# Probabilities turned, attention and spatial gating moved to joint places between the gate blocks of a macaron decoder layer

## The chip, the cores and the metric

The kernel runs on one core of a Trainium2 chip. The metric is the device time of one execution in microseconds (us); of several executions the median is given. A profile is one execution with the hardware profiler on; its span runs from the first to the last instruction.

## What is computed

A layer of a decoder on 256 tokens of 1024 features, in float32: a SwiGLU feed-forward, a token mixer with two branches, a second feed-forward and a last norm. Only the mixer matters here:

```python
n = rmsnorm(h, mix_norm[l])
z = n @ w_in[l]                                  # q, k, v, and the two halves of the gating
attn = moba_attention(q, k, v)                   # 8 heads of 64, causal softmax over 256 keys
gm = chunked_spatial_gating(zg[..., :512], zg[..., 512:], ln_g, ln_b, w_s, b_s)
y_attn = attn @ w_branch_attn[l]
y_gmlp = gm @ w_branch_gmlp[l]
gates = jax.nn.sigmoid(n @ w_gate[l] + b_gate[l])
merged = gates[..., :D] * y_attn + gates[..., D:] * y_gmlp
h = h + merged @ w_out[l]
```

## The kernel before, in words

**Products.** Every float32 weight is split into a high and a low part of 12 significant bits (`split`: a cast on ACT, L176, and a subtraction on DVE, L177), and so are the activations; a product is high x high, high x low and low x high. `by_weights` makes one block of 128 features for all 256 tokens: eight steps over the 1024 input features, each of two matmuls in `mm_side`, one of 512 columns (L159, both activation parts side by side) and one of 256 (L155). Its result is one PSUM bank with two sides. `collect` adds the sides: ACT copies one side to a small buffer `lo` (L172, two such buffers), and DVE adds the other to it (L173). Only then is the bank free.

**Banks.** All results in PSUM come from one pool, `psum`, of eight banks with one tag: `bank(name)` hands them out in turn, so each tile waits until the tile eight before it has been read.

**Weights** come in units of 1 MB, each loaded in two halves by SP into a ring of three raw buffers, split, and kept in a ring of five split units; `unit(i)` asks for loads up to three units ahead.

**Order.** The order on PE and on SP is the order of the program's text, written by hand. On DVE, ACT and POOL a scheduler sets the order; each engine then works strictly in that order.

**The stage around the change.** The scores of both token tiles (six banks `sc`, L468) come first. DVE adds the causal mask (L475) and finds the maxima (L478), ACT takes the exponentials (L483, 8 for tile 0 and 8 for tile 1), and DVE scales them by the reciprocal sums (L486, L488) in place: the probabilities. Meanwhile PE begins the sixteen gate blocks, f = 0 to 15: `gate_block(f)` is one `by_weights` (tile `pgate`), a `collect` into `gz`, a scaling (L495) and a sigmoid (L496). Between the gate blocks the loop puts smaller work on PE:

- `spatial(gp)`, gp 0 to 3: four small float32 matmuls into one bank `mix` (L532), then on DVE the bias (L535) and the product with u (L538) and a `split` into `gmT`.
- `turn(hp)`, hp 0 to 3 (two heads each): six transposes of probabilities into two banks `pk` (L505 to L507), which ACT (L509) and DVE (L511) copy to two tiles `pT`.
- `attend(hp)`: eight products of `pT` with the values into one bank `po` (L520, L522), then a `split` into `aoT`.

Before, `spatial` stood behind gates 1, 3, 5 and 7, `turn(0)` ahead of gate 7, and `attend(hp)` with `turn(hp + 1)` behind gates 8, 10 and 12; `attend(3)` stood between gates 14 and 15. The branches (L553 on) follow gate 15: for each of eight blocks one bank `pb`, its left half from `aoT` (twelve matmuls), its right half from `gmT` (twelve), then the two products with the gates, their sum and a `split`.

Of the kernel before, what the change touches and what calls it, by code (L numbers as in the profile page):

```python
# [18 lines left out]
P = 128  # L19
# [22 lines left out]
def block_kernel(ctx, tc, t, out):  # L42
# [12 lines left out]

    # The residual stream, tokens on partitions.
    h = act.tile([P, NT, D], F32, tag="h", name="h")
# [5 lines left out]

    # Until it comes, the first block of the transposed input, behind the first norm's gains.
    x0 = h[:, 0, :KB + S]
# [5 lines left out]
    eps = consts.tile([P, 1], F32, name="eps")  # L71
    nc.vector.memset(eps, EPS)
    # The activation table and the tensor engine's clock come up while the first loads run.
    warm = small.tile([P, 1], F32, tag="warm", name="warm", bufs=1)
# [6 lines left out]

    # ---- weights: loaded once, in the order in which they are used, and split
    # exactly into two float32r parts of 12 significant bits each.
    units = []
# [27 lines left out]

    # The first units wait for their split where the first hidden layer will be.
    staging = [act.tile([P, FB, S], F32, tag=f"aT{p}", name=f"stage{p}") for p in "hl"]
# [9 lines left out]
    def load_rows(i, k, end):  # L124
        """Rows k..end of a unit, loaded and split."""
        name, u = units[i]
        raw = (stage(i, k, end - k) if i < STAGED else
               rawp.tile([P, end - k, t[name].shape[-1]], F32, tag="raw", name=f"raw{i}_{k}"))
        nc.sync.dma_start(raw, t[name][u][:, k:end, :])
        w = parts[i]  # L130
        split(w[:, k:end, 0, :], w[:, k:end, 1, :], raw)
# [12 lines left out]

    # ---- float32 products of parts: high x high, high x low and low x high.
    def mm_side(ps, st, both, first, last):
        """ps[:, :n] takes high x high, ps[:, n:] the two mixed products.

        both: the moving operand's parts side by side."""
        sh, sl = st  # L150
        n = both.shape[-1]
        m = both.rearrange("p two n -> p (two n)")

        def low():
            nc.tensor.matmul(ps[:, n:], sl, both[:, 0, :], start=False, stop=False)  # L155

        if last:
            low()
        nc.tensor.matmul(ps, sh, m, start=first, stop=last)  # L159
        if not last:  # L160
            low()
# [7 lines left out]
    def collect(to, ps):  # L169
        """The sum of the sides of mm_side's bank."""  # L170
        lo = tmp.tile([P, S], F32, tag="lo", name="lo")
        nc.scalar.copy(lo, ps[:, S:])  # L172
        nc.vector.tensor_add(to, ps[:, :S], lo)  # L173
# [5 lines left out]
    def alloc_T(name, tags):  # L179
        """Feature-major activations of 1024 features: two tiles of four blocks, each in parts."""  # L180
        return [act.tile([P, 4, 2, S], F32R, tag=tag, name=f"{name}{c}") for c, tag in enumerate(tags)]
# [7 lines left out]
    def put_T(nT, src, j, half):  # L189
        """Features 4*half.. of one token tile's [P, 512] src into nT."""  # L190
        ps = bank(f"tr{j}{half}")
        for b in range(4):
            nc.tensor.transpose(ps[:, b * P:(b + 1) * P], src[:, b * P:(b + 1) * P], ident)
        tk = slice(j * P, (j + 1) * P)
        split(nT[half][:, :, 0, tk], nT[half][:, :, 1, tk], ps.rearrange("p (b t) -> p b t", b=4))
# [9 lines left out]
    def square_sum(hh, j, hf, name):  # L205
        """The sum of squares of half of each token's features."""
        if hf == 0:
            sums[name, j] = small.tile([P, 2], F32, tag="ss", name=f"ss{name}{j}")
        sq = tmp.tile([P, 512], BF16, tag="sq", name=f"sq{name}{j}{hf}", bufs=1)
        nc.scalar.activation(sq, hh[:, j, hf * 512:(hf + 1) * 512], AF.Square,  # L210
                             accum_out=sums[name, j][:, hf:hf + 1])

    def rstd_of(j, name):
        """1 / sqrt(mean(x^2) + eps) of each token of a tile."""
        ss = sums.pop((name, j))
        ms = small.tile([P, 1], F32, tag="ms", name=f"ms{name}{j}")
        nc.vector.tensor_add(ms, ss[:, 0:1], ss[:, 1:2])
        nc.vector.tensor_scalar(ms, ms, 1.0 / D, EPS, op0=ALU.mult, op1=ALU.add)
        r = small.tile([P, 1], F32, tag="rstd", name=f"rstd{name}{j}")
        nc.gpsimd.tensor_tensor(r, ms, nhalf, op=ALU.pow)  # L220
        return r

    def rows_of(rs, name):
        """The tokens' factors along the free axis, on every partition."""
        ps = bank(f"rows{name}")
# [6 lines left out]
    def by_weights(name, i, nT, blk):  # L232
        """A bank's two sides of [feature, token], 128 columns of unit i."""
        ps, w = bank(name), unit(i)
        c = slice(blk * P, (blk + 1) * P)
        for k in range(KB):
            mm_side(ps, (w[:, k, 0, c], w[:, k, 1, c]), both_of(nT, k), k == 0, k == KB - 1)
        return ps

    def by_tokens(name, i, nT, j):  # L240
        """A bank's two sides of [token, column], unit i for token tile j."""
        ps, w = bank(name), unit(i)
# [7 lines left out]
    def down(i0, n_units, part_of, scale, hh, name, done, put=None, following=(), cuts=(HALVES, HALVES)):  # L250
        """hh + scale * (a @ w), one token tile after the other at the end.

        done(new, j, cut) follows each cut of a token tile's features, put(j, cut) turns
        it over for the next product, whose first matmuls are in following."""
        acc = {(j, c0): bank(f"acc{name}{j}{c0}") for j in range(NT) for c0, n in cuts[j]}
# [38 lines left out]
    def gate_up(aT, gu, rows, name, f):  # L294
        """aT block f of silu(g) * u; g and u lie side by side in gu, to be scaled by rows."""
        nc.vector.tensor_mul(gu, gu, rows[:, None, :].to_broadcast([P, 2, S]))  # L296
# [12 lines left out]

    # ---- first feed-forward  # L310
    nT = alloc_T("n1", ("nA", "nB"))
# [15 lines left out]

    # The first units come block after block with the input.
    for i in range(2):
# [31 lines left out]

    # Constants of the mixing layer.
    bgate = consts.tile([P, 2 * KB], F32, name="bgate")
# [17 lines left out]
    def to_norm(nT, gain, rs, name):  # L381
        """What follows the parts of the residual stream on their way into the next norm."""
        hg = {}
# [18 lines left out]

    # ---- mixing
    mix_a = act.tile([P, FB, S], F32, tag="aTh", name="mix_a")
# [50 lines left out]

    # Scores of each token tile against the keys up to its own, and their softmax.
    for j in range(NT):
# [4 lines left out]
        for a0 in range(0, HEADS // 2, per):  # L462
            # Heads of different rows of the array write different banks.
            pair = [bank(f"sc{j}{a0}{two}") for two in range(2)]
# [24 lines left out]

    # Gates: sigmoid(n @ w_gate + b), features on partitions.  # L490

# [8 lines left out]
    def turn(hp):  # L500
        """The probabilities of heads 2*hp and 2*hp+1, keys on partitions."""
        pk0, pk1 = bank(f"pk0{hp}"), bank(f"pk1{hp}")
# [11 lines left out]
    def attend(hp, t0, t1):  # L514
        """The heads' probabilities times their values."""
        po = bank(f"po{hp}")
# [9 lines left out]
    def spatial(gp):  # L526
        """Groups 2*gp and 2*gp+1 of the gating, both chunks."""
        ps = bank(f"mix{gp}")
# [10 lines left out]
        split(gmT[:, gp, 0, :], gmT[:, gp, 1, :], m2)  # L539

    for f in range(2 * KB):
        if f >= 7 and f % 2 == 1 and f < 15:
            turned = turn((f - 7) // 2)
        gate_block(f)
        if f >= 8 and f % 2 == 0:
            attend(f // 2 - 4, *turned)
        if f % 2 == 1 and f < 8:
            spatial(f // 2)

    # Branches, merged by the gates.  # L550
    mT = alloc_T("mg", ("nA", "nB"))
    for f in range(KB):
        i = mb + 2 * (f // 4)  # L553
        ps = bank(f"pb{f}")
        c = slice(f % 4 * P, (f % 4 + 1) * P)
        for q, bT in enumerate((aoT, gmT)):
            w = unit(i + q)
# [23 lines left out]

    # ---- second feed-forward and the last norm
    aT, aT_block = ffn_alloc("f2")
# [21 lines left out]
    def done3(new, j, i):  # L605
        c0, n = last_cuts[j][i]
        sl = slice(c0, c0 + n)
        if i == 0:
            o[j] = act.tile([P, 2 * D], F32, tag=f"n{'CD'[j]}", name=f"o{j}")
        # Squares of x / 32: their sum is the mean over the 1024 features.  # L610
        ss = small.tile([P, 1], F32, tag="ss", name=f"ss4{j}{i}")
# [24 lines left out]
def _packed(inputs):  # L636
    """The inputs, each weight laid out unit after unit as the kernel loads it."""
    def cols(w, k, c):
# [47 lines left out]
```

## Time and profile before

| what | before |
|---|---|
| time, median of 3 runs | 556.17 us (551.77 to 558.6) |
| span of the profiled execution | 553.5 us |
| PE busy in it | 539.8 us (98%) |
| DVE busy | 394.1 us (71%) |
| ACT busy | 308.4 us (56%) |
| DMA, mean | 186 GB/s |

The profile gives the profiled execution's span alone, 553.5 us, with no time of its own around it; it lies within the runs shown. Each engine has its own queue and works it in order; a wait of PE is shown behind its row as `[idle before <-releaser]`. Matmuls overlap: the time that one adds is the distance between the starts of two rows, not the length of one.

### The profile page before, as it was taken

What the parts mean: (1) busy time and instruction counts of PE and PEld (TensorE: products, weight loads), DVE (VectorE), ACT (ScalarE), POOL (GpSimd) and SP (SyncE); (2) the same over time, 40 slices, a digit from 0 to 9 for tenths busy, and PEclk for the clock granted to TensorE, in tenths of its full rate; (3) what the DMA queues carried; (4) which work ended last, traced back from release to release, by engine and by line L of the source; (5) the groups of instructions that cost most, each with busy time, mean ns of one, the idle gap of its engine ahead of it and who ended that gap; (6) DMA issues with size and microseconds to landing.
All of it is one profiled execution on the core that took longest, in us unless ns stands there. A gap on an engine that the chain in (4) does not pass through costs nothing.

```text
span 553.5 us, 8102 instructions
## 1 busy us (share of the span) xinstructions
PE 539.8 (98%) x3042; PEld 464.2 (84%) x3042; DVE 394.1 (71%) x623; ACT 308.4 (56%) x541; POOL 10.8 (2%) x25
## 2 busy tenths in 40 slices
PE   7999999999999899999999999999999999999995
PEld 5888888888888788888878898888888888888884
DVE  5688888767745674887888777778787787866304
ACT  6666666555544454645977634575555655554203
POOL 0000000000000010000000000000000000000002
PEclk9999999999999999999999999999999999999999
DMA  8756675656767636556146545555655456556302
GB/s 254 316 174 213 210 236 178 194 181 212 252 225 235 221 125 225 188 188 206 60 142 209 183 142 196 197 190 185 200 189 187 153 178 204 195 188 229 111 0 77
DMA packets 30150, 103.03 MB, mean 186 GB/s; under 512 B 3488, under 2 KB 4256, under 8 KB 30112
## 3 DMA queue, kind: packets, MB, share of 16 engines
q1 hardware_dynamic: 30112, 102.52, 56.1%
q8 instruction: 24, 0.39, 0.3%
q14 instruction: 14, 0.11, 0.1%
HBM read 101.46 MB, written 1.05 MB: 185 GB/s over the span
## 4 chain that ended last, share of the span: by engine, by line
PE 49%; DMA 23%; DVE 15%; ACT 8%; issue 3%; SPq 1%; POOL 0%; POOLq 0%; DVEq 0%; ACTq 0%
DVE w L177 8%; PE f2u L159 7%; PE f2g L159 7%; DMA raw<-in_f1g 6%; ACT w L176 6%; DMA raw<-in_f1d 6%; PE acch L165 5%; PE acch L166 5%; PE acch L167 5%; DMA raw<-in_gate 4%; PE f2u L155 4%; PE f2g L155 4%; DMA raw<-in_qk 3%; PE pgate L159 2%; PE f L159 2%
## 5 line engine op out<-in xcount | busy, mean ns | idle before, releaser
L177 DVE TENSOR_TENSOR w<-raw,w 128x1024 fp32r<-128x1024 f32 x176 | 212.9, 1222 | 87.1 <-ACT w L176 86.5
L176 ACT CAST w<-raw 128x1024 fp32r<-128x1024 f32 x176 | 182.2, 1051 | 108.5 <-DMA raw<-in_f1d 17.6
L159 PE MATMUL f2g<-n,w 128*128 128x512 f32 x160 | 58.4, 399 | 0.0
L159 PE MATMUL f2u<-n,w 128*128 128x512 f32 x160 | 58.1, 397 | 0.0
L159 PE MATMUL f1g<-n,w 128*128 128x512 f32 x144 | 52.5, 399 | 0.0
L159 PE MATMUL f1u<-n,w 128*128 128x512 f32 x144 | 52.4, 397 | 0.0
L159 PE MATMUL pgate<-n,w 128*128 128x512 f32 x128 | 46.5, 405 | 0.7 <-DVE uz L173 0.7
L298 ACT ACTIVATE sgf<-guf 128x256 f32<-128x256 f32 x38 | 15.9, 417 | 48.3 <-DVE guf L296 48.3
L155 PE MATMUL f2u<-n,w 128*128 128x256 f32 x160 | 41.7, 281 | 0.0
L155 PE MATMUL f2g<-n,w 128*128 128x256 f32 x160 | 41.6, 281 | 0.0
L166 PE MATMUL acch<-w,f2h 128*128 128x512 f32 (+1 forms) x110 | 38.3, 349 | 0.0
L165 PE MATMUL acch<-w,f2h 128*128 128x512 f32 (+1 forms) x110 | 38.3, 348 | 0.0
L167 PE MATMUL acch<-w,f2l 128*128 128x512 f32 (+1 forms) x110 | 38.1, 347 | 0.0
L155 PE MATMUL f1u<-n,w 128*128 128x256 f32 x144 | 37.6, 281 | 0.0
L155 PE MATMUL f1g<-n,w 128*128 128x256 f32 x144 | 37.5, 281 | 0.0
L159 PEld LDWEIGHTS f2u<-n,w 128*128 128x128 f32 x160 | 30.2, 189 | 5.4
L159 PEld LDWEIGHTS f2g<-n,w 128*128 128x128 f32 x160 | 30.1, 188 | 5.5
L165 PE MATMUL acch<-w,f1h 128*128 128x512 f32 x88 | 34.3, 390 | 0.0
L167 PE MATMUL acch<-w,f1l 128*128 128x512 f32 x88 | 34.2, 389 | 0.0
L166 PE MATMUL acch<-w,f1h 128*128 128x512 f32 x88 | 34.2, 389 | 0.0
L155 PE MATMUL pgate<-n,w 128*128 128x256 f32 x128 | 33.3, 281 | 0.0
L155 PEld LDWEIGHTS f2u<-n,w 128*128 128x128 f32 x160 | 30.2, 189 | 1.9
(191 smaller groups left out, 1101.8 us busy)
## 6 DMA issues: line engine op xcount, KB each, us to landing
raw<-in_f1d SPq DMA_DIRECT2D x22, 512.0 KB, 4.6
raw<-in_f2g SPq DMA_DIRECT2D x22, 512.0 KB, 3.8
raw<-in_f2u SPq DMA_DIRECT2D x22, 512.0 KB, 4.9
raw<-in_f2d SPq DMA_DIRECT2D x22, 512.0 KB, 4.1
raw<-in_f1g SPq DMA_DIRECT2D x18, 512.0 KB, 4.6
raw<-in_f1u SPq DMA_DIRECT2D x18, 512.0 KB, 4.8
raw<-in_gate SPq DMA_DIRECT2D x16, 512.0 KB, 4.8
raw<-in_qk SPq DMA_DIRECT2D x8, 512.0 KB, 5.7
```

Of the source, the lines that this page charges most:

```text
L155: nc.tensor.matmul(ps[:, n:], sl, both[:, 0, :], start=False, stop=False)
L159: nc.tensor.matmul(ps, sh, m, start=first, stop=last)
L165: nc.tensor.matmul(ps, sh, mh, start=first, stop=False)
L166: nc.tensor.matmul(ps, sh, ml, start=False, stop=False)
L167: nc.tensor.matmul(ps, sl, mh, start=False, stop=last)
L176: nc.scalar.copy(hi, src)
L177: nc.vector.tensor_sub(lo, src, hi.bitcast(F32))
L298: nc.scalar.activation(sg, gu[:, 0, :], AF.Silu)
```

## The change

The four `spatial` calls go to two places: 0 and 1 ahead of gate 2, 2 and 3 ahead of gate 4. `turn(0)` goes from ahead of gate 7 to ahead of gate 8, and the pairs `attend(hp)`, `turn(hp + 1)` from behind gates 8, 10, 12 to ahead of gates 10, 12, 14, one block later each; `attend(3)` stays between gates 14 and 15. In the branches the `gmT` half is multiplied first. Nothing is added to or taken from the computation. (The diff also drops comments and docstrings, which shifts line numbers behind L540 by 8.)

```diff
+    turned = {}
+
+    def turn_next(hp):
+        turned[hp] = turn(hp)
+
+    def attend_next(hp):
+        attend(hp, *turned.pop(hp))
+
+    between = {2: [(spatial, 0), (spatial, 1)], 4: [(spatial, 2), (spatial, 3)], 8: [(turn_next, 0)],
+               10: [(attend_next, 0), (turn_next, 1)], 12: [(attend_next, 1), (turn_next, 2)],
+               14: [(attend_next, 2), (turn_next, 3)], 15: [(attend_next, 3)]}
     for f in range(2 * KB):
-        if f >= 7 and f % 2 == 1 and f < 15:
-            turned = turn((f - 7) // 2)
+        for step, i in between.get(f, ()):
+            step(i)
         gate_block(f)
-        if f >= 8 and f % 2 == 0:
-            attend(f // 2 - 4, *turned)
-        if f % 2 == 1 and f < 8:
-            spatial(f // 2)
...
-        for q, bT in enumerate((aoT, gmT)):
+        for q, bT in ((1, gmT), (0, aoT)):
             w = unit(i + q)
```

On PE, gates 1 to 5 before (the first row of a block stands for its sixteen matmuls; `x4` is the four matmuls of one `spatial`; the number behind a name only keeps tiles apart):

```order
L159 MATMUL pgate1_2553<-n21_1466,w43_2258 128x512
L532 MATMUL mix0_2575<-wsT_1457,mix_a_1948 64x128 x4
L159 MATMUL pgate2_2587<-n20_1465,w44_2332 128x512
...
L159 MATMUL pgate3_2619<-n20_1465,w44_2332 128x512
...
L532 MATMUL mix1_2641<-wsT_1457,mix_a_1948 64x128 x4
L159 MATMUL pgate4_2653<-n20_1465,w45_2387 128x512
...
L159 MATMUL pgate5_2685<-n20_1465,w45_2387 128x512
...
L532 MATMUL mix2_2707<-wsT_1457,mix_a_1948 64x128 x4
```

and after:

```order
L159 MATMUL pgate1_2553<-n21_1466,w43_2258 128x512
L532 MATMUL mix0_2575<-wsT_1457,mix_a_1948 64x128 x4
L532 MATMUL mix1_2586<-wsT_1457,mix_a_1948 64x128 x4
L159 MATMUL pgate2_2598<-n20_1465,w44_2332 128x512
...
L159 MATMUL pgate3_2630<-n20_1465,w44_2332 128x512
...
L532 MATMUL mix2_2652<-wsT_1457,mix_a_1948 64x128 x4
L532 MATMUL mix3_2663<-wsT_1457,mix_a_1948 64x128 x4
L159 MATMUL pgate4_2675<-n20_1465,w45_2387 128x512
```

Counted from gate 0, the ninth bank asked for was that of `mix2`, behind gate 5; now it is that of gate 4.

On DVE, ahead of and at the copy of turned probabilities that `attend(0)` needs (`pT10`), before:

```order
L173 TENSOR_TENSOR gz4_2652<-pgate4_2653,lo_2679 128x256
L173 TENSOR_TENSOR gz5_2684<-pgate5_2685,lo_2702 128x256
L495 TENSOR_TENSOR gz4_2652<-gz4_2652,rowsb2_2099 128x256
L177 TENSOR_TENSOR ag1_2519<-gm1_2648,ag1_2519 128x256
L495 TENSOR_TENSOR gz5_2684<-gz5_2684,rowsb2_2099 128x256
L535 TENSOR_TENSOR mixb2_2712<-mix2_2707,bs_1454 128x256
L177 TENSOR_TENSOR w49_2720<-raw49_4_2725,w49_2720 128x4x256
L538 TENSOR_TENSOR gm2_2714<-mixb2_2712,mix_b_1949 128x256
L173 TENSOR_TENSOR gz6_2718<-pgate6_2719,lo_2745 128x256
L511 COPY pT10_2760<-pk10_2751 128x256
```

and after:

```order
L538 TENSOR_TENSOR gm3_2670<-mixb3_2668,mix_b_1949 128x256
L495 TENSOR_TENSOR gz4_2674<-gz4_2674,rowsb2_2099 128x256
L173 TENSOR_TENSOR gz5_2706<-pgate5_2707,lo_2724 128x256
L177 TENSOR_TENSOR w50_2798<-raw50_0_2799,w50_2798 128x4x256
L177 TENSOR_TENSOR ag1_2519<-gm3_2670,ag1_2519 128x256
L495 TENSOR_TENSOR gz5_2706<-gz5_2706,rowsb2_2099 128x256
L173 TENSOR_TENSOR gz6_2729<-pgate6_2730,lo_2756 128x256
L511 COPY pT10_2794<-pk10_2785 128x256
```

The copy still stands right behind the collect of gate 6 (`gz6`), but all four `spatial` results and one more half unit of weights (`w50`) are now ahead of it. From the collect of gate 0 (`gz0`) to this copy DVE had four weight splits and 21 smaller instructions; it now has five and 25. Ahead of `gz0` DVE and ACT have the same instructions in the same order as before.

## Rows read from the trace of the kernel before

**Rows 1.** The page: span, and engines by busy time, share and instructions.
```profile
span 553.5 us, 8102 instructions
PE 539.8 (98%) x3042; PEld 464.2 (84%) x3042; DVE 394.1 (71%) x623; ACT 308.4 (56%) x541; POOL 10.8 (2%) x25
```

**Rows 2.** Who PE waited for, two of seven: us in total, times, longest.
```profile
PE tr L193 <- DVE hg L200: 1.6, 2, 0.9
...
PE pgate L159 <- DVE uz L173: 0.7, 1, 0.7
```

**Rows 3.** Timeline of PE, gates 0 to 4: start, length, instruction.
```profile
260.26 0.63 PE L159 MATMUL pgate<-n,w 128*128 128x512 f32 x2
...
263.08 0.39 PE L159 MATMUL pgate<-n,w 128*128 128x512 f32 x1
263.40 0.66 PE L532 MATMUL mix<-wsT,mix_a 128*64 128x128 f32 x8
263.99 0.50 PE L159 MATMUL pgate<-n,w 128*128 128x512 f32 x1
...
269.82 0.66 PE L532 MATMUL mix<-wsT,mix_a 128*64 128x128 f32 x8
270.41 0.50 PE L159 MATMUL pgate<-n,w 128*128 128x512 f32 x1
```

**Rows 4.** Timeline of PE around `attend(0)`, `attend(1)` and `attend(3)`.
```profile
286.96 0.40 PE L159 MATMUL pgate<-n,w 128*128 128x512 f32 x1
287.65 0.65 PE L520 MATMUL po<-pT,mix_b 128*64 128x256 f32 x2 [0.29 <-ACT pT L509]
289.11 0.32 PE L522 MATMUL po<-pT,mix_b 128*64 128x128 f32 x1 [0.81 <-DVE pT L511]
...
290.54 0.47 PE L159 MATMUL pgate<-n,w 128*128 128x512 f32 x1
...
296.02 0.39 PE L159 MATMUL pgate<-n,w 128*128 128x512 f32 x1
...
297.78 0.47 PE L159 MATMUL pgate<-n,w 128*128 128x512 f32 x1
...
310.91 0.66 PE L520 MATMUL po<-pT,mix_b 128*64 128x256 f32 x4
```

**Rows 5.** Timeline of DVE: collects of gates 0 and 1, splits, copies, a branch.
```profile
275.24 0.75 DVE L173 TENSOR_TENSOR gz<-pgate,lo 128x256 f32<-128x256 f32 x2
...
276.57 2.36 DVE L177 TENSOR_TENSOR w<-raw,w 128x1024 fp32r<-128x1024 f32 x2
...
288.63 0.42 DVE L511 COPY pT<-pk 128x256 f32<-128x256 f32 x1
...
307.77 0.42 DVE L511 COPY pT<-pk 128x256 f32<-128x256 f32 x1
...
323.49 0.42 DVE L561 TENSOR_TENSOR m<-pb,mix_a 128x256 f32<-128x256 f32 x1 [0.77 <-PE pb L167]
```

**Rows 6.** Windows: busy PE, PEld, DVE, ACT, POOL; granted PE clock; DMA share, GB/s.
```profile
12.00:16.00 4.00, 4.00 (x17) 3.44 (x16) 3.69 (x8) 3.04 (x7) 0.00 (x0) 0.57 1.04 412
...
192.00:196.00 4.00, 3.30 (x18) 2.71 (x19) 3.71 (x8) 2.86 (x7) 0.55 (x1) 1.00 0.36 122
...
548.00:552.00 4.00, 0.00 (x0) 0.00 (x0) 0.90 (x3) 0.80 (x3) 0.74 (x2) 0.92 0.34 131
```

**Rows 7.** Timeline of PE in the first feed-forward's first blocks (`f`).
```profile
10.34 0.50 PE L159 MATMUL f<-n,w 128*128 128x512 f32 x1 [2.56 <-ACT w L176]
...
13.02 0.41 PE L155 MATMUL f<-n,w 128*128 128x256 f32 x1
...
13.66 0.41 PE L155 MATMUL f<-n,w 128*128 128x256 f32 x1
...
15.87 0.28 PE L155 MATMUL f<-n,w 128*128 128x256 f32 x1
...
16.21 0.28 PE L155 MATMUL f<-n,w 128*128 128x256 f32 x1
```

## The prediction

> **What bounds the kernel now.** I read the page first: PE is busy 98% of the 553.5 us span, DVE 71%, ACT 56% [rows 1]. So PE sets the time, and what matters is only how long PE stands still or works more slowly. Second I read the list of what PE waited for. It has seven rows. Two name weights, and both lie in the first blocks of the first feed-forward; from there on PE never waits for a weight. The two waits at the turns into a new norm, 1.6 us together [rows 2], follow from PE's own work and move with it. So whatever PE gains or loses among the gates reaches the end of the kernel in full. Third I read PE's timeline through the gates. The places where the loop leaves the gate blocks show as steps in the starts, and two waits stand at `attend(0)` [rows 4]. Fourth I read DVE over the same stretch, for the time at which it frees PE's banks [rows 5], and last the granted clock in windows, since a longer wait of PE can lower it [rows 6, 7].
>
> **The joint places.** The unbroken step from the last matmul of one gate to the next is 0.23 us: the pair of rows at 260.26 is 0.63 long where one alone is 0.40 [rows 3]. From the last matmul of gate 1 (263.08) to the first of gate 2 (263.99) it is 0.91, so a `spatial` with its two changes of work costs 0.68. Its eight matmuls take 0.66 in all, 0.27 of it the last one's length (the row's 0.66 against steps of about 0.056), so the second `spatial` in a place adds 8 x 0.056 = 0.45, not 0.68. Two places are saved: 2 x 0.23 = **-0.46 us**. `turn` and `attend` stand in as many places as before (five), so they give nothing here.
>
> **The bank of gate 4.** The pool has eight banks in turn. That a tile really waits for the eighth before it shows at gate 0, which waited 0.7 us for DVE to collect a `pu` block [rows 2]: two `pu`, six `sc`, gate 0. Counted from gate 0, the ninth tile was `mix2`; PE came to it only after gate 5, when the collect of gate 0 was over. Now the first eight are gates 0 to 3 and all four `mix`, and the ninth is gate 4. PE gets there early. Gate 2 starts 0.45 later than at 263.99, at 264.44; gates 2 and 3 take the 5.83 us from 263.99 to 269.82 [rows 3], so `mix2` starts at 270.27; 0.59 (269.82 to 270.41) and 0.45 more, and gate 4 is due at 271.31. The collect of gate 0 starts at 275.24 and takes 0.42 [rows 5]. It stands behind the softmax, and nothing ahead of it on DVE or ACT has moved, nor waits for PE: the bank is free at 275.66. A wait of PE ends about 0.06 later (the copy from 288.63 to 289.05 released the row at 289.11 [rows 4, 5]). PE waits from 271.31 to 275.72: **+4.41 us**. Behind gate 4 stands everything on PE. Gates 5, 6 and 7 need the banks of gate 1 and of the first two `mix`, which DVE reads within some 4 us of 275.24, ahead of PE.
>
> Here a rule speaks the other way. Perfetto Trace Analysis in the Trainium skill, section Optimizing Tensor Performance, Matmuls, says that independent groups should rotate through different banks, so that the evacuation of one overlaps the next group's matmuls. The kernel still rotates; by the rule alone the 4.41 would be nothing and the sum -2.28. The rows show that rotation hides an evacuation only as long as the ring holds a free bank, and here it comes round 4.4 us too soon.
>
> **The wait at `attend(0)`.** From the last matmul of gate 8 (286.96, plus the step of 0.23) to the first of gate 9 (290.54) `attend(0)` and `turn(1)` took 3.35 us; the same pair after gate 10, without a wait, took 297.78 - 296.25 = 1.53 [rows 4]. So the wait, for copies that came at 288.63 on DVE, cost 1.82. After the change DVE has five weight splits (1.14 apart: two in 2.36, of which the last is 1.22) and 25 small ones (0.33 apart) from `gz0` to that copy, 13.95 us, which is 289.2 without a wait. Before, four and 21 made 11.5, and the copy came 1.9 later than that [rows 5]; with the same delay it now starts at 291.1. PE comes to `attend(0)` after six gates (2.92 each, from the 5.83) and one turn from 275.72: not before 293.2. So the copy is in time: **-1.82 us**. If DVE falls behind by 2 us more, this is lost, up to 1.82.
>
> **`attend(3)`** now follows its `turn` by one gate instead of two. Before, it started at 310.91 without a wait, so its turn ended at about 310.91 - 5.83 = 305.1; the copy ended at 308.19 [rows 4, 5], 3.1 after it. One gate covers 2.92. I take **0**; the bounds are 0 and the 1.82 of `attend(0)`.
>
> **The clock.** The trace shows one wait of PE like the new one: 2.56 us before 10.34 [rows 7]. From about 12 on the granted clock is at its lower level: the window 12 to 16 has a mean of 0.57, which is (1 - 0.57) / 0.5 x 4 = 3.4 us at 1.2 instead of 2.4 GHz [rows 6]. In it a pair of matmuls took 0.64 (13.02 to 13.66), afterwards 0.34 (15.87 to 16.21) [rows 7]. 3.4 / 0.64 = 5.3 pairs, 0.30 each: 1.6 us. The 1.6 us of waits at the turn into the second norm did not lower it (1.00 from 192 to 196), and after PE's end it fell at about 551.4, over 3.4 us into the idle time [rows 6]. A wait of 4.41 is far longer than the one that sufficed, so I expect a fall near its end or shortly after: **+1.6 us**. Bounds: 0 if it doesn't fall; 1.1 if the fall comes 3.4 us into the wait, so that 1.0 of the low stretch is waited away; 3.2 if it stays low for two stretches.
>
> **The branches.** `gmT` first: the matmuls are the same, in another order; PE did not wait for `aoT` before, and DVE began with a `pb` block only after both halves (the wait of 0.77 before 323.49 [rows 5]). A unit of the attention branch is now given back twelve matmuls later, which delays the split of an output weight by 1.4 us, with units split well ahead of use. **0**; what hides it is that lead, and if that were gone the cost would be up to 1.4 for each of two units.
>
> **Sum:** -0.46 + 4.41 - 1.82 + 0 + 1.6 + 0 = **+3.7 us**. Against the profiled execution's own span, 553.5, this is 557.2. The median of the runs is 556.17, 2.7 above that span; single runs go from 551.77 to 558.6. On the median the forecast is **559.9 us**, 0.7% slower.
>
> **The rivals.**
> 1. *The stall without the clock's fall*: +2.1, 558.3. For it: clock 1.00 through every other wait after 16 us. Against it: 2.56 us sufficed once. Chance 0.17.
> 2. *Stall, clock, and late copies*: `attend(0)` still waits its 1.82, or `attend(3)` waits as long: +5.5, 561.7. For it: DVE's extra split and the short way to `attend(3)`. Against it: PE comes later, DVE works on while PE waits. Chance 0.13.
> 3. *Faster: no stall at gate 4.* If the collect of gate 0 were done when PE arrives, -0.46 - 1.82 = -2.3 remains: 553.9. The point that decides is a wait at gate 4 of under 2.28 us, so a collect over by 273.5 instead of 275.66 (and a wait so short may leave the clock alone). For it: the softmax chain ahead of the collect varies with the landing of a weight half. Against it: nothing of the change is ahead of it. Chance 0.08.
> 4. *Nothing happens*, as the stall replaces what `attend(0)` lost or is made up later: 556.2. Against it: 4.41 against 2.28, and no later wait of PE that a delay could shorten. Chance 0.04.
>
> The forecast itself has 0.58. About 2% (11 us) is what a measurement of this kernel can tell from no change. No case reaches that: the worst, 4.41 - 0.46 + 3.2 + 1.82 + 1.4, is +10.4. So same 0.96, slower 0.03, faster 0.01. For the range I take rivals 1 and 2 at its inner side, with about 3 us for the scatter that the runs before show about their median: 555.5 to 563.5. Rival 3 lies below it.
>
> **What the profile after would show.** A wait of PE ahead of gate 4 of about 4.4 us, released by DVE's collect of `gz` (L173); a `spatial` place with sixteen matmuls in about 1.1 us; no wait at `attend(0)`; a window of 3 to 4 us with the clock near 0.5 beginning near 275 to 279; the branches at the same 2.9 us a block; gate 0 to the first branch matmul 3.7 us longer than before. The prediction is wrong if gate 4 starts near 271.3 on the old scale, if the clock stays at 1.00, or if PE waits at `attend(3)`.

## The result, and the profile after

The changed kernel takes 558.2 us (median of 20 runs, 555.35 to 560.99); the kernel before took 555.29 in the same rounds. The ratio is 1.0059, with a 95% interval of 1.004 to 1.0078. Run twice more the same code gave 1.0052 and 1.0039 (below). So the change costs 0.4 to 0.6%, some 2 to 3 us: well under 2%, but clearly above nothing. The forecast was 559.9 us, 3.7 above before; rival 1, the stall without the clock's fall, stood at 558.3, so the time alone does not part the two. (Ratios are of undisturbed runs alone, so a median below stands a little off its ratio here and there.)

| what | before | after |
|---|---|---|
| median of 20 runs each | 555.29 us | 558.2 us |
| span of the profiled execution | 553.5 us | 553.3 us |
| wait of PE ahead of gate 4, in it | none | 1.29 us |
| gate 0 to the first branch matmul, in it | 57.1 us | 55.5 us |
| matmuls of `spatial` in one place, first start to last end | eight, 0.66 us | sixteen, 1.09 us |

The page of the profiled execution after, span and engines, answers to [rows 1]:

```profile
span 553.3 us, 8106 instructions
PE 538.5 (97%) x3042; PEld 463.8 (84%) x3042; DVE 394.2 (71%) x623; ACT 308.6 (56%) x541; POOL 10.6 (2%) x25
```

That span is not longer than before's. It belongs to the fastest of the 20 runs (555.35 us; a run's time is its span and 2.0 to 2.1 us in each of them), so this one trace cannot show the typical loss. Its list of what PE waited for (us in total, times, longest) has a row that before lacked, the third of these:

```profile
PE tr L193 <- DVE hg L200: 3.6, 2, 2.9
PE f L159 <- DVE n L325: 2.2, 1, 2.2
PE pgate L159 <- DVE gz L173: 1.3, 1, 1.3
```

The timeline of PE through gates 0 to 4 after (start, length, instruction) answers to [rows 3], and around `attend(0)` to [rows 4]:

```profile
258.78 0.50 PE L159 MATMUL pgate<-n,w 128*128 128x512 f32 x1
...
264.60 1.09 PE L532 MATMUL mix<-wsT,mix_a 128*64 128x128 f32 x16
265.62 0.50 PE L159 MATMUL pgate<-n,w 128*128 128x512 f32 x1
...
271.45 1.09 PE L532 MATMUL mix<-wsT,mix_a 128*64 128x128 f32 x16
273.83 0.50 PE L159 MATMUL pgate<-n,w 128*128 128x512 f32 x1 [1.29 <-DVE gz L173]
...
291.61 0.66 PE L520 MATMUL po<-pT,mix_b 128*64 128x256 f32 x4
```

The joint places stand there as sixteen matmuls in 1.09 us. Gate 4 waits for the collect of gate 0's bank, as the prediction said, but for 1.29 us and not 4.41. `attend(0)` begins without a wait; its four matmuls come in one piece. The collect on DVE and the granted clock in that stretch (windows: PE busy, clock, DMA share, GB/s) answer to [rows 5] and [rows 6]:

```profile
273.36 0.75 DVE L173 TENSOR_TENSOR gz<-pgate,lo 128x256 f32<-128x256 f32 x2
```

```profile
258.00:274.00 16.00, 14.71 (x105) 1.00 0.28 92
274.00:278.00 4.00, 4.00 (x23) 1.00 0.24 70
```

The collect starts 14.58 us behind gate 0 (258.78 to 273.36). In before's trace it started 17.67 behind it. And the clock stayed at its upper level after this wait.

The third run of the same code was profiled in an execution of about the median time. There PE's timeline, DVE's, and the windows read:

```profile
256.88 0.50 PE L159 MATMUL pgate<-n,w 128*128 128x512 f32 x1
...
269.55 1.09 PE L532 MATMUL mix<-wsT,mix_a 128*64 128x128 f32 x16
274.14 0.50 PE L159 MATMUL pgate<-n,w 128*128 128x512 f32 x1 [3.49 <-DVE gz L173]
...
275.04 0.41 PE L155 MATMUL pgate<-n,w 128*128 128x256 f32 x1
...
275.68 0.41 PE L155 MATMUL pgate<-n,w 128*128 128x256 f32 x1
...
279.17 0.28 PE L155 MATMUL pgate<-n,w 128*128 128x256 f32 x1
...
279.52 0.28 PE L155 MATMUL pgate<-n,w 128*128 128x256 f32 x1
```

```profile
273.66 0.75 DVE L173 TENSOR_TENSOR gz<-pgate,lo 128x256 f32<-128x256 f32 x2
```

```profile
274.00:278.00 4.00, 3.86 (x13) 0.57 0.15 42
278.00:282.00 4.00, 4.00 (x25) 1.00 0.67 223
```

This is the picture of the prediction: a wait of 3.49 us for the collect of gate 0, not quite the 4.41, and soon after gate 4 begins the clock falls to 1.2 GHz. A pair of matmuls takes 0.64 (275.04 to 275.68) instead of 0.35 (279.17 to 279.52). (1 - 0.57) / 0.5 x 4 is 3.4 us at the lower level. From gate 0 to the first branch matmul this execution needs 59.2 us.

### The profile page after: what moved, and what is told of

It reads as the page before. It is cut to its first block, busy times and chain, and to the rows that moved or that the text cites. A ratio compares the mean times of both kernels' runs of the same rounds, so it can differ in the third digit from the quotient of the medians.

```text
span 553.3 us, 8106 instructions
## 1 busy us (share of the span) xinstructions
PE 538.5 (97%) x3042; PEld 463.8 (84%) x3042; DVE 394.2 (71%) x623; ACT 308.6 (56%) x541; POOL 10.6 (2%) x25
## 3 DMA queue, kind: packets, MB, share of 16 engines
q1 hardware_dynamic: 30112, 102.52, 55.5%
## 4 chain that ended last, share of the span: by engine, by line
PE 81%; DMA 7%; DVE 6%; ACT 3%; issue 1%; SPq 0%; POOL 0%; POOLq 0%; DVEq 0%; ACTq 0%
PE acch L165 8%; PE acch L166 8%; PE acch L167 8%; PE f2g L159 7%; PE f2u L159 7%; PE f1g L159 6%; PE f1u L159 6%; PE pgate L159 4%; PE f2g L155 4%; PE f2u L155 4%; DMA raw<-in_qk 3%; PE f1u L155 3%; PE f1g L155 3%; DVE w L177 3%; DMA raw<-in_gate 2%; PE f L159 2%
```

## The experiments

Three theories were put against each other. By the *ring theory*, that of the prediction, the loss is the wait of gate 4 for gate 0's bank and the clock that falls in it. By the *late-turns theory* it is `turn` and `attend` standing a block later. By the *chance theory* the clock falls at places that have nothing to do with the gates. "Low-clock time" is worked out from each run's span and mean granted clock c as 2 (1 - c) x span: the time at 1.2 GHz when the rest is at 2.4. It is given over the runs that the ratio counts. A run's mean clock does not say where in the kernel the clock fell; that only a trace shows.

| kernel | median us | runs | ratio to before, 95% | low-clock us, mean |
|---|---|---|---|---|
| changed, first | 558.20 | 20 | 1.0059 [1.004, 1.0078] | 10.6 |
| changed, again | 557.95 | 12 | 1.0052 [1.0018, 1.0087] | 10.3 |
| changed, third | 557.06 | 12 | 1.0039 [1.0017, 1.006] | 9.7 |
| gatings joined alone | 556.16 | 12 | 1.0024 [0.9988, 1.006] | 9.0 |
| turns late alone | 555.73 | 12 | 1.0047 [1.0006, 1.0089] | 7.0 |
| changed, gatings at gates 6 and 7 | 555.38 | 12 | 0.9997 [0.9962, 1.0032] | 5.2 |
| changed, paired halves of a bank | 553.67 | 12 | 0.9993 [0.9964, 1.0023] | 6.2 |
| the same again | 555.62 | 12 | 0.9979 [0.9943, 1.0015] | 6.3 |
| paired halves, turns as before | 554.54 | 12 | 0.9973 [0.994, 1.0006] | 7.0 |
| changed, the wait filled | 556.05 | 12 | 1.0022 [0.9991, 1.0053] | 5.2 |
| before, ring shortened by two | 559.24 | 12 | 1.0044 [1.0005, 1.0082] | 7.9 |
| changed, ring shortened by three | 562.27 | 6 | 1.0112 [1.0071, 1.0154] | 14.6 |
| before, against itself | 554.19 | 12 | 1.0018 [0.999, 1.0047] | 5.3 |

The kernel before has a mean of 6.7 us of low-clock time over 108 runs, those of the last row among them. The last row says how far a ratio can be from 1 by chance here: differences of 0.002 are not to be read. Low-clock time scatters too: before has 6.8 to 7.0 in three sets of runs and 5.3 in the fourth. Behind the first row there are three sets of runs of before. Beside the first stood the changed kernel again, the two halves and the late gatings; beside the second the changed kernel's third run, the first of the paired halves, the filled wait and before itself; beside the third the two shortened rings, the paired halves again and those with the turns as before.

**The changed kernel again, and its two halves.**

> The changed kernel once more, for a second trace of it and the granted clock of every run. Ring theory (mine): gate 4 is the ninth bank of the ring and waits for the collect of gate 0; the first trace of the changed kernel, its fastest execution, showed 1.3 us of that wait at clock 1.00, so slower executions must show a longer one (up to 4.4 us) and, where it is long, a stretch of 3.4 us at the lower clock behind it: ratio to before 1.006, mean clock of the slow runs 0.003 below that of the fast ones for each such stretch. Rival (late-turns theory: the delay comes from turn and attend standing a block later and from attend(3) only one gate behind its turn): waits at po, none over 1.5 us at gate 4, ratio 1.006. Rival (chance theory: the clock falls elsewhere, at the turn into the second norm, as in that first trace): before has as many runs at a lowered clock as this.

> Only the four spatial calls stand in their two joint places; turn, attend and the order of the branch halves are those of before. Ring theory: the ninth bank is that of gate 4 as in the change, so the wait at gate 4 and the fall of the clock stay; attend(0) keeps its 1.8 us at most: ratio 1.006 to 1.010 (+3.5 to +5.5 us). Late-turns theory: nothing of the delay is here: ratio 0.999 (-0.5 us). Chance theory: ratio 0.999 to 1.001.

```diff
-    between = {2: [(spatial, 0), (spatial, 1)], 4: [(spatial, 2), (spatial, 3)], 8: [(turn_next, 0)],
-               10: [(attend_next, 0), (turn_next, 1)], 12: [(attend_next, 1), (turn_next, 2)],
-               14: [(attend_next, 2), (turn_next, 3)], 15: [(attend_next, 3)]}
+    between = {2: [(spatial, 0), (spatial, 1)], 4: [(spatial, 2), (spatial, 3)], 7: [(turn_next, 0)],
+               9: [(attend_next, 0), (turn_next, 1)], 11: [(attend_next, 1), (turn_next, 2)],
+               13: [(attend_next, 2), (turn_next, 3)], 15: [(attend_next, 3)]}
...
-        for q, bT in ((1, gmT), (0, aoT)):
+        for q, bT in enumerate((aoT, gmT)):
```

> Only turn and attend stand a block later, as in the change; spatial 0 to 2 stand as before, spatial 3 ahead of gate 8 beside turn(0); the branch halves in the order of before. Ring theory: mix2 behind gate 5 is the ninth bank as before, no wait at gate 4; the 1.8 us at attend(0) go: ratio 0.9965 (-2.0 us). Late-turns theory: the whole delay is here: ratio 1.006. Chance theory: 0.9965 to 1.

```diff
-    between = {2: [(spatial, 0), (spatial, 1)], 4: [(spatial, 2), (spatial, 3)], 8: [(turn_next, 0)],
+    between = {2: [(spatial, 0)], 4: [(spatial, 1)], 6: [(spatial, 2)], 8: [(spatial, 3), (turn_next, 0)],
...
-        for q, bT in ((1, gmT), (0, aoT)):
+        for q, bT in enumerate((aoT, gmT)):
```

The changed kernel repeated its ratio here, and once more in its third run (expected below). Its trace had a wait of 0.86 us ahead of gate 4 and no fall of the clock. The halves went against the ring theory: 1.0024 with the gatings alone, where it had 1.006 to 1.010, and 1.0047 with the turns alone, where it had 0.9965, below the whole interval. Both intervals hold what the late-turns theory expected (0.999 and 1.006). They are wide and overlap, and with the turns alone the medians differ by 0.6 us only (555.73 against 555.10), so the ratios of the halves settle nothing. But their traces differ. With the gatings alone PE's timeline and the windows show the wait and the fall once more:

```profile
268.22 1.09 PE L532 MATMUL mix<-wsT,mix_a 128*64 128x128 f32 x16
271.79 0.50 PE L159 MATMUL pgate<-n,w 128*128 128x512 f32 x1 [2.47 <-DVE gz L173]
```

```profile
271.00:273.00 2.00, 1.22 (x7) 1.00 0.00 0
273.00:277.00 4.00, 4.00 (x16) 0.57 0.44 135
```

With the turns alone there is no wait at the gates, and from gate 0 to the first branch matmul it takes 55.7 us, against 58.1 with the gatings alone. Its low-clock time is that of before (7.0), while the gatings alone have 9.0.

**The gatings late.** The changed kernel with the joint places ahead of gates 6 and 7, so that the ninth bank comes later.

> The changed kernel with its two joint places of spatial moved back: 0 and 1 ahead of gate 6, 2 and 3 ahead of gate 7. Ring theory: the first eight banks are those of gates 0 to 5 and two mix, the ninth is that of gate 6, which PE reaches at about 276, when the collect of gate 0 is over: no wait there, clock 1.00, and the joint places and attend(0) keep their gain: ratio 0.996 (-2.3 us). Late-turns theory: the delay stays: ratio 1.006. Chance theory: 0.996 to 1.

```diff
-    between = {2: [(spatial, 0), (spatial, 1)], 4: [(spatial, 2), (spatial, 3)], 8: [(turn_next, 0)],
+    between = {6: [(spatial, 0), (spatial, 1)], 7: [(spatial, 2), (spatial, 3)], 8: [(turn_next, 0)],
```

The loss is gone from the ratio (0.9997) with the turns left late, and the low-clock time is back, though the 0.996 that the ring theory had did not come. Its trace shows no wait at gates 6 and 7, but one behind them, for a bank of a gating:

```profile
284.28 0.50 PE L159 MATMUL pgate<-n,w 128*128 128x512 f32 x1 [0.84 <-DVE mixb L535]
```

With this and late copies at `attend(0)`, `attend(2)` and `attend(3)` that execution takes 57.8 us from gate 0 to the first branch matmul, so the one trace is not free of loss. The run speaks for the ring, but it moves the gatings too; the next one moves nothing on PE.

**Paired halves.** TensorE's order is that of the changed kernel, matmul for matmul; two gatings share a bank.

> The changed kernel, except that the two spatial gatings of a joint place write the two halves of one bank instead of a bank each. TensorE's order is that of the changed kernel, matmul for matmul; only the ring of banks differs: the ninth tile counted from gate 0 is now gate 6, not gate 4. Ring theory (the loss comes from gate 4, which waits for the bank of gate 0, and from the clock that falls in that wait): no wait of TensorE ahead of gate 4, low-clock time back at that of the kernel before (some 7 to 8 us a run instead of 10 to 11), and the gains of the joint places and of attend(0) are left, so 0 to 2.3 us faster than before, ratio 0.996 to 1.000. Late-turns theory (turn and attend a block later cost the time, whatever the banks do): about 2 us slower, as the kernel with the turns alone was, ratio 1.003 to 1.005. Chance theory (the loss comes from clock falls that have no tie to the gates): as the changed kernel, ratio 1.005.

> The paired halves with late turns once more, beside the others. Ring theory: ratio 0.997 to 1.001, no wait ahead of gate 4, low-clock time 5.5 to 7.5 us a run, as in its first 12 runs (0.9993 and 6.2 us). Late-turns theory: 1.003 or more, which its first runs have all but ruled out.

```diff
-    def spatial(gp):
-        ps = bank(f"mix{gp}")
-        for j in range(NT):
+    def spatial(g0):
+        ps = bank(f"mix{g0}")
+        for gp in (g0, g0 + 1):
+            c0 = (gp - g0) * S
+            for j in range(NT):
...
-    between = {2: [(spatial, 0), (spatial, 1)], 4: [(spatial, 2), (spatial, 3)], 8: [(turn_next, 0)],
+    between = {2: [(spatial, 0)], 4: [(spatial, 2)], 8: [(turn_next, 0)],
```

Ratios 0.9993 and 0.9979, low-clock time 6.2 and 6.3. Against the changed kernel, third run, beside it that is 557.06 - 553.67 = 3.4 us (2.9 between the means). Some 0.3 us of it lies outside the span: a run's time is 1.7 us over its span in the paired kernel and 2.05 in the changed one, for a reason that no trace shows. PE's timeline of the first of the two shows gate 4 right behind the sixteen small matmuls, and then something at `attend(3)`:

```profile
269.52 1.09 PE L534 MATMUL mix<-wsT,mix_a 128*64 128x128 f32 x16
270.55 0.50 PE L159 MATMUL pgate<-n,w 128*128 128x512 f32 x1
...
308.48 0.65 PE L520 MATMUL po<-pT,mix_b 128*64 128x256 f32 x2 [0.64 <-ACT pT L509]
309.26 0.32 PE L522 MATMUL po<-pT,mix_b 128*64 128x128 f32 x1
```

DVE's copy for it comes late as well:

```profile
308.78 0.42 DVE L511 COPY pT<-pk 128x256 f32<-128x256 f32 x1
```

So the loss hung on which tile was the ninth: with PE's order unchanged it is gone, to within the intervals. The late-turns theory, which had 1.003 or more for both runs, falls as an explanation of it. What it had right is smaller: with the stall gone, `attend(3)`, one gate behind its `turn`, waits for its copies. From the first row of gate 14 to that of gate 15 the paired kernel took 3.70 + 1.58 = 5.28 us in this trace and 4.85 in the other, the changed kernel 2.99 + 0.80 = 3.79: a loss of 1.5 and 1.1. The kernel with the turns alone has it too (3.35 + 1.57, a loss of 1.1), which is somewhat under half of its ratio of 1.0047 (2.6 us). The rest, some 1.5 us, is not explained; before against itself was off by 0.0018, or 1.0 us. Part of such differences arises ahead of the stage: gate 0 starts between 253.28 and 261.67 us in the fourteen traces, though up to there all kernels do the same.

**Paired halves, turns as before.**

> The kernel with paired halves of a bank, with turn and attend in the places that the kernel before had (turn(0) ahead of gate 7, then a joint place every second gate). What is left of the change is the two joint places of the gatings, without the bank, and the order of the branches. Ring theory: the joint places give 0.46 us and nothing else moves, ratio 0.997 to 1.001. Late-turns theory: faster than the paired halves with late turns by about 1.9 us.

```diff
-    between = {2: [(spatial, 0)], 4: [(spatial, 2)], 8: [(turn_next, 0)],
-               10: [(attend_next, 0), (turn_next, 1)], 12: [(attend_next, 1), (turn_next, 2)],
-               14: [(attend_next, 2), (turn_next, 3)], 15: [(attend_next, 3)]}
+    between = {2: [(spatial, 0)], 4: [(spatial, 2)], 7: [(turn_next, 0)],
+               9: [(attend_next, 0), (turn_next, 1)], 11: [(attend_next, 1), (turn_next, 2)],
+               13: [(attend_next, 2), (turn_next, 3)], 15: [(attend_next, 3)]}
```

0.9973 [0.994, 1.0006]: the lowest ratio of all, still not shown to be under 1. It beats the changed kernel (its interval ends below where that kernel's three begin), and it is not told apart from before, nor from the paired halves with late turns (0.9979 beside it), where the late-turns theory had 1.9 us between them. The wait at `attend(3)` is gone, and in its trace `attend(0)` takes 0.8 us longer for a late copy (1.63 from its start to that of the next turn, against 0.81 where nothing waits).

**The wait filled.** 24 matmuls of zeros behind `spatial(3)`, into columns that nobody reads.

> The changed kernel with 24 matmuls of zeros (256 columns each, into the unread half of the bank of spatial(3); they add nothing to the result) put behind spatial(3), where TensorE would wait for the bank of gate 4. They take some 2.6 us, so they fill the wait where it is that long and push gate 4 back where it is shorter. Ring theory with the clock: the stall stays in full, but TensorE works through it, so the clock does not fall there: low-clock time 7 to 8 us a run instead of 10 to 11, and the time 0.5 to 1.5 us under the changed kernel, ratio to before 1.002 to 1.004. If the clock has no part in the loss: low-clock time as in the changed kernel, and the time 0 to 1.5 us above it, ratio 1.005 to 1.008. If the stall is nothing but chance: 2.6 us above the changed kernel, ratio 1.010.

```diff
+        if gp == 3:
+            for _ in range(24):
+                nc.tensor.matmul(ps[:, S:], zeros[:, :P], zeros, start=True, stop=True)
```

PE's timeline, DVE's collect and the windows:

```profile
265.95 1.09 PE L532 MATMUL mix<-wsT,mix_a 128*64 128x128 f32 x16
266.98 2.79 PE L536 MATMUL mix<-zeros 128*128 128x256 bf16 x24
269.52 0.48 PE L159 MATMUL pgate<-n,w 128*128 128x512 f32 x1
```

```profile
268.93 0.75 DVE L173 TENSOR_TENSOR gz<-pgate,lo 128x256 f32<-128x256 f32 x2
```

```profile
266.00:270.00 4.00, 4.00 (x44) 1.00 0.00 0
270.00:274.00 4.00, 4.00 (x25) 1.00 0.33 101
```

The zeros took 2.54 us of PE (266.98 to 269.52), about as long as the wait would have been (the collect ends at 268.93 + 0.42). Gate 4 is no earlier, but the low-clock time is 5.2 us instead of 9.7, and the median is 1.0 us under the changed kernel's beside it (the means differ by 1.9, with a standard error of 0.8). The clock stays at 1.00 there. One trace shows little, since of the waits of this length some were not followed by a fall either (last section); the low-clock time of all runs is the evidence that filling the wait keeps the clock. By the times, the clock is then 1 to 2 us of the loss of 2.9 to 3.4, and the stall itself the rest. (Where the wait would have been shorter, the zeros push gate 4 back, so the clock's share is larger than this if anything.)

**The stall put into the kernel before.** Before's order, with two banks of the ring held back.

> The kernel before, in its own order, with the ring of banks shortened by two: after gate 2 two banks are taken, each written by one small matmul of zeros, and given back by two one-column products on VectorE after gate 7, whose result nothing reads. So gate 4 is the ninth tile from gate 0 and waits for gate 0's bank, as in the changed kernel, with nothing else of the change there. Ring theory: a wait of TensorE ahead of gate 4 of 1.3 to 4.4 us released by the collect of gz (in the changed kernel three traces had 0.9, 1.3 and 3.5; gate 4 is due 0.9 sooner here), a clock that falls there in some executions, low-clock time 9 to 11 us a run, and a time 2.5 to 4.5 us above before, ratio 1.0045 to 1.008. Chance theory and late-turns theory: as before, ratio 0.999 to 1.002, low-clock time 6 to 7.5 us.

```diff
+        if f == 2:
+            skip = [bank("skip0"), bank("skip1")]
+            for b in skip:
+                nc.tensor.matmul(b[:, :P], zeros[:, :P], zeros[:, :P], start=True, stop=True)
+        if f == 7:
+            for b in skip:
+                nc.vector.tensor_mul(seen, b[:, :1], gates[:, 0, :1])
```

**The stall made longer.** The changed kernel with three banks held back from behind gate 1 in the same way: gate 3 becomes the ninth.

> The changed kernel with three more banks taken after gate 1 and given back after gate 7 in the same way, so that gate 3 is the ninth tile and waits for gate 0's bank. Gate 3 is due some 3.9 us sooner than gate 4 (one gate block of 2.9 and a joint place of 1.0). Ring theory: the wait is 3.9 us longer than in the changed kernel (4.5 to 7.5 in a trace), it ends at the same collect, the clock falls in nearly every execution, and later places wait up to 1 us for banks of their own: 4 to 5 us above the changed kernel, ratio to before 1.011 to 1.015. Late-turns theory, by which the early banks do not matter: as the changed kernel, 1.004 to 1.006.

```diff
+        if f == 2:
+            skip = [bank(f"skip{i}") for i in range(3)]
+            for b in skip:
+                nc.tensor.matmul(b[:, :P], zeros[:, :P], zeros[:, :P], start=True, stop=True)
```

PE's timeline and windows, of the first:

```profile
273.25 0.66 PE L532 MATMUL mix<-wsT,mix_a 128*64 128x128 f32 x8
277.05 0.50 PE L159 MATMUL pgate<-n,w 128*128 128x512 f32 x1 [3.14 <-DVE gz L173]
```

```profile
277.00:281.00 4.00, 3.95 (x13) 0.57 0.13 47
281.00:285.00 4.00, 4.00 (x29) 1.00 0.64 215
```

and of the second:

```profile
270.58 0.40 PE L159 MATMUL pgate<-n,w 128*128 128x512 f32 x1
277.25 0.79 PE L159 MATMUL pgate<-n,w 128*128 128x512 f32 x1 [6.28 <-DVE gz L173]
```

```profile
271.00:275.00 4.00, 0.00 (x0) 0.96 0.00 0
275.00:279.00 4.00, 1.75 (x5) 0.50 0.00 0
279.00:283.00 4.00, 4.00 (x28) 0.69 0.55 172
```

The stall alone makes before 1.0044 times as long, within the changed kernel's 1.0039 to 1.0059; the longer stall gives 1.0112, or 562.27 - 555.98 = 6.3 us. In time both came out at the low end of what the ring theory had in advance (the first just under its 1.0045); no later place waited for a bank. One mark missed: the first has 7.9 us of low-clock time (9.8 over all twelve runs), where the ring theory had 9 to 11 and the chance theory 6 to 7.5, and its trace, with the fall in it, is of a long execution (561.42 us). Chance and late turns had 0.999 to 1.002 for the first, which its interval, from 1.0005 on, does not quite leave behind; late turns had 1.004 to 1.006 for the second, which lies below its interval.

**The kernel before against itself.**

> The kernel before once more, against itself. All theories: ratio 1.000 within 0.002; a ratio off by as much as 0.003 would show that differences of that size between the others are not to be told from none. It also gives a second execution of the kernel before with a trace: by the ring theory the time from gate 0 to the collect of gz0 differs between executions (17.7 us in the first trace of the kernel before, 14.6 in that of the changed kernel) by what the cast of a weight half waits for its DMA.

> The changed kernel once more, on the same chip as the paired banks and the filled wait, so that these can be compared with it directly. Ring theory: ratio 1.004 to 1.007, a wait of TensorE ahead of gate 4 of 0.9 to 4.4 us, low-clock time 10 to 11 us a run. Chance theory: ratio 1.000 to 1.005 with low-clock time anywhere from 7 to 11 us.

The second trace of before is the most useful row of this study. PE's start of gate 0, its `attend(0)`, and DVE's collect:

```profile
258.36 0.50 PE L159 MATMUL pgate<-n,w 128*128 128x512 f32 x1
...
287.52 0.66 PE L520 MATMUL po<-pT,mix_b 128*64 128x256 f32 x4
```

```profile
273.96 0.75 DVE L173 TENSOR_TENSOR gz<-pgate,lo 128x256 f32<-128x256 f32 x2
```

There is no wait at `attend(0)`, and the collect starts 15.60 us behind gate 0, not 17.67 as in the trace that the prediction had ([rows 5] less the start of gate 0). From gate 0 to the first branch matmul it took 54.6 us, against 57.1. By this measure, which leaves out all that differs ahead of the gates, the changed kernel has 55.5, 55.1 and 59.2, the paired halves 56.1 and 55.2 (with the turns as before 54.9), and the shortened rings 59.6 and 62.7.

## Why the prediction was right

The sign, the mechanism and its place held; the size, +3.7 against a measured +2 to +3, came out near because two terms were too large by one and the same cause.

- **The joint places, -0.46: held.** Gate 0 to the first branch matmul is 54.6 us in the second trace of before, without a wait. In the changed kernel it is, less the waits inside: 55.1 - 0.86 = 54.2 (again), 55.5 - 1.29 = 54.2 (first). The saving is 0.4.
- **The bank of gate 4, +4.41: right in kind, mis-sized.** The working fixes when gate 4 is due relative to gate 0, and adds the collect's start. The first half is exact: by it a collect that starts L behind gate 0 gives a wait of L - 17.67 + 4.41. With L of 16.78, 15.77, 14.58 and 14.15 in the four traces (third, gatings alone, first, again) that is 3.52, 2.51, 1.32 and 0.89; measured were 3.49, 2.47, 1.29 and 0.86. What failed is L. It was taken from one execution, and that was the longest of fourteen: the thirteen others have 14.15 to 16.78, mean 15.8, so a wait of 2.5 us would have been the term. DVE's chain from its first mask addition (L475) to the collect is 13.8 to 13.9 us in all thirteen and 14.4 in that one. What varies is how far DVE is behind PE when gate 0 starts (0.3 to 3.2 us). In the first trace of before a cast on ACT waited 1.28 us for a weight half there; what else sets this lag was not tried. The prediction named it as what speaks for rival 3, and gave it a chance but no place in the term. By rival 3's own mark, a wait of under 2.28 us, two of the changed kernel's three traces were its case; the kernel was not faster all the same, since the 1.82 that it counted on was not there to be gained.
- **The wait at `attend(0)`, -1.82: wrong as a gain.** That it vanishes was right. But it belongs to late executions: before's other trace has no such wait. A DVE that is 2 us late makes the stall at gate 4 long and `attend(0)` wait, so both terms grew together, with opposite signs, and the sum stayed near: -0.46 + 2.5 + 0 + 1.6 would have been +3.6. That they offset each other was luck, not working.
- **`attend(3)`, 0 with a bound of 1.82: held because of the stall.** In the changed kernel's three traces it does not wait. In the kernels without the stall, and the turns as late, it loses 1.1 to 1.5 us. DVE and ACT work on while PE stands at gate 4; take the stall away and the cover is gone. This, and the 1.82 at `attend(0)` that a typical execution does not have to gain, is why the paired kernels' expected gain of up to 2.3 did not come. Moving `attend(3)` behind gate 15 on top of the paired halves is the obvious next version; it was not run.
- **The clock, +1.6: held, though not in every execution.** Where it falls, the gates that run at the lower level cost 1.53 (third run: four gates in 12.91 us, against 11.38 elsewhere), 1.5 (gatings alone) and 1.6 (stall put into before). In two of the changed kernel's three traces it did not fall, after waits of 0.86 and 1.29. Over all runs the changed kernel has 10.3 us of low-clock time (44 runs) against 6.7: 3.6 us more, as much as one stretch of 3.4 an execution. That these lie at the gates is shown by the trace of the third run, and for the rest argued from the kernels without the stall, which have 5.2 to 7.0.
- **The branches, 0: held.** Eight blocks take 23.0 us in every trace, and from the first branch matmul to the end of the span it is 238.7 to 239.0 us in all fourteen, with either order of the halves. So what is lost or gained among the gates does reach the end in full, as the prediction said.
- **The weighed rule** (Perfetto Trace Analysis in the Trainium skill, Optimizing Tensor Performance, Matmuls: let independent groups rotate through different banks). By it alone the sum was -2.28. The paired kernel, which uses fewer banks, is 3.4 us faster than the changed one, which gives each gating its own: here a bank for each small group cost the time, since the ring came round before its first bank was read.
- **A sum in the bounds.** The worst case, +10.4, takes the 1.4 of the branches once, though the prediction gives it for each of two units. With both it is +11.8, over the 11 us that it says no case reaches. Nothing measured comes near it.

Of the marks named in advance, the wait, its releaser, the joint places, `attend(0)` and the branches came as told; the low clock did in one trace of three; gate 0 to the first branch matmul is 0.9, 0.4 and 4.6 us longer than in the undelayed trace of before (first, again, third), not a fixed 3.7. By the prediction's own sign of being wrong, a clock that stays at 1.00, two of three traces failed it; so its picture holds for the late executions, not for each.

## What to carry to other kernels

Before results are moved together ahead of a block, count the pool's tiles from the last one that is read late: the tile that takes its bank waits for it, however far its own work is from it. Two small results that are read together can share one bank; here this cost nothing that the runs could tell (0.9993 and 0.9979 to before). A wait at a point where two engines run at their own pace is worth what several executions show: one trace gave 4.41 here where the mean of thirteen others gives 2.5, and a second term of the same sum carried the same error with the other sign.

## What the runs showed of the hardware

The clock did not answer alike to like waits. The turn into the second norm has a wait of PE of up to 3.6 us ahead of its transposes. PE's timeline and the windows in the second trace of before:

```profile
191.90 0.63 PE L193 MATMUL tr<-ident,hg 128*128 128x128 f32 x4 [2.40 <-DVE hg L200]
```

```profile
194.00:196.00 2.00, 2.00 (x7) 0.51 0.07 25
```

and in the first of the paired kernel:

```profile
191.97 0.63 PE L193 MATMUL tr<-ident,hg 128*128 128x128 f32 x4 [2.39 <-DVE hg L200]
```

```profile
194.00:196.00 2.00, 2.00 (x10) 1.00 0.04 8
```

The same wait to 0.01 us, and a fall in one only. In the traces of this study waits of up to 1.64 us at this place and at the gates were not followed by a fall; of four between 2.39 and 2.49 two were; all of 2.87 and more were, some within 1.8 us behind the wait's end, some inside the wait. The wait of 6.28 us is one of those: the clock stayed low for about two stretches (windows of 271 to 283: 0.3 + 4 + 2.5 us at the lower level), and some 2.5 us of them passed while PE stood still. What passes while PE waits slows no matmul, so the loss is not in proportion to the low-clock time. Nor does the low stretch go by the wait's length: around a wait of 3.00 us at the same turn, in the second trace of the paired kernel, the clock was as long at its lower level, from about 193.8 to 200.6.
